# One broadcast tensor_tensor multiply in place of eight tensor_scalar multiplies in a grouped softmax

## The chip, the cores and the metric

One core of one Trainium2 chip. The metric is the device time of one execution in microseconds, lower is better. A profile is one execution taken by the hardware profiler; its span, from first to last instruction, is about 2 us shorter than the device time. A run counts as slow when it takes over 1.5% more than the fastest of the same kernel; the others are called fast. Of a kernel run only once the state is unknown.

## The reference

A softmax over groups: each row of 4352 numbers is eight groups of 544, and each group is normalised by itself.

```python
B, N, D, G = 4, 4096, 4352, 8           # x is float32
def reference(x):
    Dg = D // G                          # 544
    x_g = x.reshape(B, N, G, Dg)
    x_g = x_g - x_g.max(axis=-1, keepdims=True)
    exp = np.exp(x_g)
    out = exp / exp.sum(axis=-1, keepdims=True)
    return out.reshape(B, N, D)
```

Input and output are 285 MB each.

## The kernel before

The 16384 rows are cut into 128 tiles of 128 rows. A tile is loaded by one DMA of 2.2 MB, worked on in place and stored by one DMA. VectorE (DVE) finds the eight maxima, ScalarE (ACT) does the exponentials and their sums, DVE takes the reciprocals and scales. Twelve tile buffers are in use; all transfers go out in order from the queue of SyncE (SP).

```python
NBUF = 12
pool = ctx.enter_context(tc.tile_pool(name="io", bufs=NBUF))
small = ctx.enter_context(tc.tile_pool(name="small", bufs=4))
# ...
def expo(i):
    xt = tiles[i]
    mx = small.tile([P, G], f32, name="mx")
    nc.vector.reduce_max(out=mx, in_=xt, axis=mybir.AxisListType.X, negate=True)   # L45
    # ... eight activations (Exp, bias=mx of the group, accum_out=sm of the group)  # L49

def scale(i):
    xt = tiles[i]
    rs = small.tile([P, G], f32, name="rs")
    nc.vector.reciprocal(out=rs, in_=sums.pop(i))                                   # L61
    for g in range(G):
        nc.vector.tensor_scalar_mul(out=xt[:, g, :], in0=xt[:, g, :], scalar1=rs[:, g:g + 1])  # L63

AHEAD = NBUF - 2
with tc.manual_schedule():
    for i in range(AHEAD):
        load(i)                          # L37
    for i in range(nt + 1):
        if i < nt:
            expo(i)
        if i:
            scale(i - 1)
            store(i - 1, nc.sync)        # L40
            if i - 1 + AHEAD < nt:
                load(i - 1 + AHEAD)
```

## Time and profile before

| | before |
|---|---|
| device time, median of 3 runs | 1342.13 us (1341.66 to 1342.44) |
| span of the profile | 1340.1 us |
| DVE busy | 1046.7 us, 78% |
| ACT busy | 764.3 us, 57% |
| moved | 570.44 MB, 431 GB/s in the steady part |

How to read the lines below. A row of a group of instructions has: source line, engine, operation, output<-input by name, then by shape, count | busy us in all, mean ns of one | idle us of the engine just before them and what ended most of it. The digits after "DMA" are the busy share of the transfer engines in tenths, in 40 equal slices of the span. The lines themselves stand in the prediction.

### The profile page before, as it was taken

To read this page: it belongs to the slowest core of one execution; us is meant where nothing else is said; L and a number is where in the kernel's file an instruction comes from. 1 tells how busy PE (TensorE), PEld (TensorE's weight loads), DVE (VectorE), ACT (ScalarE), POOL (GpSimd) and SP (SyncE) were. 2 spreads that over 40 slices of the span, in tenths; PEclk is the share of its full clock that TensorE was granted. 3 is DMA by queue.
4 is the path that set the end of the run, shared out by engine and by line. 5 is a ranking of instruction groups with operands and counts; after the bars stand their busy time and mean duration, and the time that the engine had idled before them with its cause. 6 is when DMAs were issued, how large, how long until landed. Compare 5 with 4: busy or idle time off the path is not lost.

```text
span 1340.1 us, 4119 instructions
## 1 busy us (share of the span) xinstructions
DVE 1046.7 (78%) x1280; ACT 764.3 (57%) x2049; POOL 0.2 (0%) x4
## 2 busy tenths in 40 slices
DVE  6999987878777887888777877778877887777760
ACT  5777766555655565556555556555665556555540
POOL 0000000000000000000000000000000000000000
DMA  9999999999999999999999999999999999999996
GB/s 399 426 429 431 430 430 432 432 432 431 431 432 430 432 431 432 431 431 431 431 430 431 432 430 432 431 430 431 431 432 430 432 431 429 430 431 431 430 432 266
DMA packets 36896, 570.70 MB, mean 426 GB/s; under 512 B 4096, under 2 KB 4096, under 8 KB 4096
## 3 DMA queue, kind: packets, MB, share of 16 engines
q1 hardware_dynamic: 36864, 570.44, 99.4%
q14 instruction: 32, 0.26, 0.0%
HBM read 285.21 MB, written 285.21 MB: 426 GB/s over the span
## 4 chain that ended last, share of the span: by engine, by line
DMA 88%; DVE 7%; SPq 1%; ACT 1%; issue 1%; DVEq 0%; ACTq 0%
DMA out_dram<-xt 85%; DVE mx L45 4%; DVE xt L63 3%; DMA xt<-in_x_dram 3%; SPq L37 1%; ACT xt L49 1%; DVE rs L61 0%; DVEq L104 0%; ACTq L104 0%
## 5 line engine op out<-in xcount | busy, mean ns | idle before, releaser
L49 ACT ACTIVATE xt<-xt,mx 128x544 f32<-128x544 f32 x1024 | 751.2, 735 | 524.3 <-issue 435.8
L45 DVE TENSOR_REDUCE mx<-xt 128x8 f32<-128x4352 f32 x128 | 599.6, 4685 | 247.6 <-DMA xt<-in_x_dram 247.6
L63 DVE TENSOR_SCALAR xt<-xt,rs 128x544 f32<-128x544 f32 x1024 | 434.2, 498 | 4.5
L49 ACT ACTIVATION_READ_ACCUMULATOR xt<-xt,mx 128x1 f32 x1024 | 191.3, 187 | 0.0
L61 DVE RECIPROCAL rs<-sm 128x8 f32<-128x8 f32 x128 | 24.7, 193 | 3.4 <-ACT xt L49 3.4
L49 ACT ACT_TABLE_LOAD x1 | 1.3, 1283 | 9.9 <-DMA xt<-in_x_dram 9.9
L93 POOL MEMSET const-bfloat16-1.0<- 128x1 bf16 x1 | 0.1, 101 | 0.0
L93 POOL MEMSET const-uint8-127<- 128x1 uint8 x1 | 0.1, 101 | 0.0
L93 POOL MEMSET const-float32-0.0<- 128x1 f32 x1 | 0.1, 98 | 0.2 <-issue 0.2
L93 POOL MEMSET const-float32-1.0<- 128x1 f32 x1 | 0.1, 98 | 0.0
## 6 DMA issues: line engine op xcount, KB each, us to landing
xt<-in_x_dram SPq DMA_DIRECT2D x128, 2176.0 KB, 25.8
out_dram<-xt SPq DMA_DIRECT2D x128, 2176.0 KB, 30.6
```

The lines of the kernel that those rows point to most:

```text
L37: nc.sync.dma_start(out=xt, in_=xg[i * P:(i + 1) * P])
L45: nc.vector.reduce_max(out=mx, in_=xt, axis=mybir.AxisListType.X, negate=True)
L49: nc.scalar.activation(out=xt[:, g, :], in_=xt[:, g, :], func=mybir.ActivationFunctionType.Exp, bias=mx[:, g:g + 1], scale=1.0, accum_out= ...
L61: nc.vector.reciprocal(out=rs, in_=sums.pop(i))
L63: nc.vector.tensor_scalar_mul(out=xt[:, g, :], in0=xt[:, g, :], scalar1=rs[:, g:g + 1])
L93: nc = _bacc.Bacc("TRN2", target_bir_lowering=False, num_devices=1)
```

## The change

The intent is fewer instructions: 128 multiplies in place of 1024. The reciprocals `rs` (128x8) are read as if they were 128x8x544, each repeated along its group.

```diff
-    def scale(i):
-        xt = tiles[i]
+    def scale(i, r):
+        xr = row(i, r)
         rs = small.tile([P, G], f32, name="rs")
-        nc.vector.reciprocal(out=rs, in_=sums.pop(i))
-        for g in range(G):
-            nc.vector.tensor_scalar_mul(out=xt[:, g, :], in0=xt[:, g, :], scalar1=rs[:, g:g + 1])
+        nc.vector.reciprocal(out=rs, in_=sums.pop((i, r)))
+        nc.vector.tensor_mul(
+            out=xr, in0=xr, in1=rs.unsqueeze(2).to_broadcast([P, G, Dg]))
```

The rest of the diff (cut here) rewrites the loops so that a tile could hold several rows a partition. With `R = 1`, as it stands, the tiles, transfers and order are the ones of before.

More of the change, by code (lines that the diff above doesn't have):

```diff
@@ L18 @@
     P = 128
+    R = 1
     NBUF = 12
@@ L23, with rows, store, row @@
     Dg = D // G
-    xg = xf.rearrange("n (g d) -> n g d", g=G)
-    og = of.rearrange("n (g d) -> n g d", g=G)
-    nt = N // P
+    f32 = mybir.dt.float32
     pool = ctx.enter_context(tc.tile_pool(name="io", bufs=NBUF))
     small = ctx.enter_context(tc.tile_pool(name="small", bufs=4))
-    f32 = mybir.dt.float32
+    spans = []
+    at = 0
+    while at < N:
+        r = min(R, (N - at) // P)
+        spans.append((at, r))
+        at += r * P
+    nt = len(spans)
     tiles = {}
     sums = {}
+    def rows(dram, i):
+        at, r = spans[i]
+        return dram[at:at + r * P].rearrange("(p r) d -> p (r d)", r=r)
     def load(i):
-        xt = pool.tile([P, G, Dg], f32, name="xt")
+        xt = pool.tile([P, R * D], f32, name="xt")
         tiles[i] = xt
-        nc.sync.dma_start(out=xt, in_=xg[i * P:(i + 1) * P])
-    def store(i, eng):
-        eng.dma_start(out=og[i * P:(i + 1) * P], in_=tiles.pop(i))
-    def expo(i):
-        xt = tiles[i]
+        nc.sync.dma_start(out=xt[:, :spans[i][1] * D], in_=rows(xf, i))
+    def store(i):
+        nc.sync.dma_start(out=rows(of, i), in_=tiles[i][:, :spans[i][1] * D])
+    def row(i, r):
+        return tiles[i][:, r * D:(r + 1) * D].rearrange("p (g d) -> p g d", g=G)
+    def expo(i, r):
+        xr = row(i, r)
         mx = small.tile([P, G], f32, name="mx")
-        nc.vector.reduce_max(out=mx, in_=xt, axis=mybir.AxisListType.X, negate=True)
+        nc.vector.reduce_max(out=mx, in_=xr, axis=mybir.AxisListType.X, negate=True)
         sm = small.tile([P, G], f32, name="sm")
-        sums[i] = sm
+        sums[i, r] = sm
         for g in range(G):
             nc.scalar.activation(
-                out=xt[:, g, :],
-                in_=xt[:, g, :],
+                out=xr[:, g, :],
+                in_=xr[:, g, :],
                 func=mybir.ActivationFunctionType.Exp,
@@ L56, in expo @@
             )
-    def scale(i):
-        xt = tiles[i]
+    def scale(i, r):
+        xr = row(i, r)
         rs = small.tile([P, G], f32, name="rs")
-        nc.vector.reciprocal(out=rs, in_=sums.pop(i))
-        for g in range(G):
-            nc.vector.tensor_scalar_mul(out=xt[:, g, :], in0=xt[:, g, :], scalar1=rs[:, g:g + 1])
+        nc.vector.reciprocal(out=rs, in_=sums.pop((i, r)))
+        nc.vector.tensor_mul(
+            out=xr, in0=xr, in1=rs.unsqueeze(2).to_broadcast([P, G, Dg]))
     AHEAD = NBUF - 2
+    work = [(i, r) for i in range(nt) for r in range(spans[i][1])]
     with tc.manual_schedule():
@@ L70 @@
             load(i)
-        for i in range(nt + 1):
-            if i < nt:
-                expo(i)
-            if i:
-                scale(i - 1)
-                store(i - 1, nc.sync)
-                if i - 1 + AHEAD < nt:
-                    load(i - 1 + AHEAD)
+        for n in range(len(work) + 1):
+            if n < len(work):
+                expo(*work[n])
+            if n:
+                i, r = work[n - 1]
+                scale(i, r)
+                if r == spans[i][1] - 1:
+                    store(i)
+                    if i + AHEAD < nt:
+                        load(i + AHEAD)
 _INS = ['x']
```

## The prediction

> **What bounds the kernel now.** I read the page first: busy shares, the DMA rows of the 40 slices, the share of the DMA queue, and the chain that ended last.
>
> ```profile
> span 1340.1 us, 4119 instructions
> DVE 1046.7 (78%) x1280; ACT 764.3 (57%) x2049; POOL 0.2 (0%) x4
> DMA  9999999999999999999999999999999999999996
> ...
> q1 hardware_dynamic: 36864, 570.44, 99.4%
> ...
> DMA 88%; DVE 7%; SPq 1%; ACT 1%; issue 1%; DVEq 0%; ACTq 0%
> ...
> L45 DVE TENSOR_REDUCE mx<-xt 128x8 f32<-128x4352 f32 x128 | 599.6, 4685 | 247.6 <-DMA xt<-in_x_dram 247.6
> L63 DVE TENSOR_SCALAR xt<-xt,rs 128x544 f32<-128x544 f32 x1024 | 434.2, 498 | 4.5
> ```
>
> The reader is to see that the transfer engines are full in 39 of 40 slices and that the input and output (570.44 MB) take 99.4% of their time. At the 431 GB/s that the slices show, 570.44 MB are 1323.5 us; start-up and the emptying at the end are the other 17. DVE is busy 78%, and its only large idle item, 247.6 us, is spent waiting for loads: it waits for the transfers, not they for it.
>
> Whether a slower DVE would reach the transfers is decided by the queue that issues them. So next come the waits of that queue (who waited for whom: us in total, times, longest).
>
> ```profile
> SPq L37 <- DMA out_dram<-xt: 1104.5, 116, 16.7
> ...
> SPq L40 <- DVE xt L63: 13.1, 5, 4.1
> ```
>
> A load (L37) waits for the store that frees its buffer, 1104.5 us in all. A store (L40) waited for the multiply only 5 times, 13.1 us: stores are nearly always ready before their turn. How long before, the instructions of one steady tile show (start, duration, in brackets the idle time before):
>
> ```profile
> 598.20 4.69 DVE L45 TENSOR_REDUCE mx<-xt 128x8 f32<-128x4352 f32 x1 [2.08 <-DMA xt<-in_x_dram]
> 602.81 0.19 DVE L61 RECIPROCAL rs<-sm 128x8 f32<-128x8 f32 x1
> ...
> 603.03 3.39 DVE L63 TENSOR_SCALAR xt<-xt,rs 128x544 f32<-128x544 f32 x8
> ...
> 603.36 0.33 SPq L37 DMA_DIRECT2D xt<-in_x_dram  x1
> ...
> 603.74 0.46 SPq L40 DMA_DIRECT2D out_dram<-xt  x1
> ...
> 608.52 4.69 DVE L45 TENSOR_REDUCE mx<-xt 128x8 f32<-128x4352 f32 x1 [2.09 <-DMA xt<-in_x_dram]
> ```
>
> From reduce to reduce a tile takes 608.52 - 598.20 = 10.32 us, which is what the transfers need (2 x 2.228 MB at 431 GB/s = 10.34 us). DVE works 8.2 of them and idles 2.1. Counting the issues from the first one on, the load at 603.36 is that of tile 64 and the store at 603.74 that of tile 55. A load lands 25.8 us after its issue (page, DMA issues), so tile 64 is reduced at about 629.4, three periods after 598.20; the reduce at 598.20 is then tile 61, and the multiply at 603.03 works on tile 60 (each turn reduces a tile, then scales the one before). So tile 55 was scaled five periods before its store was issued: some 48 us of slack. The slack of the reduce is 2.1 us a tile and that of the store 48 us.
>
> **What the Trainium skill says.** (1) "VectorE: DVE Perf Modes", section "The perf-mode tier table": in fp32 from SBUF, tensor_scalar runs at two elements a cycle, tensor_tensor and tensor_reduce at one, since the second tensor takes the second read port. The same page's errata section gives (N+151)/0.96 ns for an fp32 tensor_tensor add. The trace agrees for what it holds: the reduce of 4352 took 4685 ns, against 4690 by that formula; a multiply of 544 took 498 ns, under the 567 that one element a cycle would cost (544/0.96), so it runs in the faster mode. The trace of before has no tensor_tensor. (2) "Perfetto Trace Analysis", section "Optimizing Scalar/DVE Operations": each DVE instruction on SBUF carries some 60 ns, and the profiled latency about twice that. The trace: eight multiplies span 3.39 us, so they start (3390 - 498)/7 = 413 ns apart, of which 283 are elements (544/2/0.96): 130 ns each, closer to the second figure. (3) "SBUF — State Buffer", section "Who interferes with whom": DMA never contends with a compute engine. The trace agrees closely: from 40 to 60 us, with DVE busy 19.93 of 20, the transfers moved 425 GB/s; at 300 to 320, with DVE at 15.75, 430; from 1303 to 1318, with no engine at work, 433. GpSimd, which shares DVE's second port by that page, is idle here.
>
> **The change, part by part.**
> Removed: 1024 multiplies, eight a tile, 8 x 413 ns = 3.31 us of DVE a tile from first start to the next instruction.
> Added: 128 tensor_tensor of 128x4352. Record by the formula (4352+151)/0.96 = 4690 ns. The reduce, with the same count, has the next instruction start 4.59 to 4.61 us after it, so I take 4.60 us on the engine (estimate). Two effects work against each other: seven fixed costs saved (7 x 0.13 = 0.91 us), and twice the cycles for the elements (4352/2/0.96 = 2.27 us more). Net about +1.3 us a tile; 4.60 - 3.31 gives 1.29. Grouping the instructions makes the work slower, because it leaves the fast mode.
> Unchanged: reduce and reciprocal, exponentials on ACT, number, size and order of transfers. In the built programs the loads' waits are the same; a store has gained a wait for the exponentials of its own tile, which end before the multiply does, so it costs nothing beyond one queue entry.
> DVE a tile: 4.60 (reduce) + 0.23 (to the multiply) + 4.60 = 9.43 us, before 8.13. That is under 10.33. Over 128 tiles: 599.6 + 24.7 + 128 x 4.60 = 1213 us, 90% of the span; DVE stays the second, not the first.
> On the path: in the steady part +1.29 comes out of the 2.1 us idle and leaves 0.8, and a store is ready 1.3 us later out of 48. Cost 0.
> Ramp: DVE begins behind the loads and works back to back. Before, tile k's reduce starts near 24.1 + 8.13(k-2), and its load lands near 88.7 + 10.33(k-12) (the load of tile 12 was issued at 62.93); these meet at k = 20, 167 us. The trace has the first such wait of more than a microsecond ending at 172.49. After: 25.4 + 9.43(k-2), which meets it at k = 46 or so, 440 us. The store of tile 3 was issued at 63.35; its multiply will now end near 53.7, and the margin grows with each tile. The first three stores go out 1 to 3.5 us later, with at least seven transfers of 5.2 us still queued ahead: no hole. Cost 0.
> Tail: the last load lands at 1287.75, the last store was issued at 1302.2 and will be at 1303.5. Transfers stay at full rate till 1324, so about four stores are queued when it comes: hidden too. The last 14 us are a few transfer engines ending late, at a fifth of the rate. Cost 0 to 1.3 us.
> Sum: 0 to +1.3 us. There may be a trifle to gain from fewer instruction fetches (0.26 MB in all). I predict 1342.3 us.
>
> **The rivals.**
> Fewer instructions, faster kernel: for it, 896 fewer records on DVE. Against it, those hide behind a full DMA, and were they all free, the floor of 1323.5 us plus the fill would still stand: less than 1% to win. Time 1339 to 1342.
> DVE becomes the bound: it needs a tensor_tensor above 10.33 - 4.83 = 5.5 us, 1.2 cycles an element. A broadcast that rereads one word 544 times, or two read streams in SBUF, might cost that; no row of before shows such an operand, and the tier table gives one a cycle. At two cycles an element, 9.1 us, a tile would take 13.9 us and the kernel some 1800.
> A wait takes the place of the removed one: a late multiply holds the store, which holds the load behind it in the same queue. Against it stand the 48 us of slack and the five waits. If it did bite in the ramp: 1345 to 1350.
> The tail shows in full: 1343.4.
> DVE's second read stream slows the transfers: with DVE at 90% at the 425 GB/s of the busiest window instead of 431, 1% or 13 us, 1355. But that window is also the ramp, where loads outnumber stores, so I give it little.
>
> **Range and chances.** The three runs of before lie within 0.8 us, so the range is about mechanism: 1339.5 (rival one) to 1346 (tail and a little of the ramp). The chance of slower by over 2% is that of a tensor_tensor above 5.7 us or so: 0.03. Faster by 2% would need more than the transfers leave: 0.01. Within 2%: 0.96.
>
> **What would show it.** Right: the tensor_tensor's row at about 4.69 us mean; DVE near 90%; the reduce's idle time down from 247.6 to some 80 us (82 tiles x 0.85 and the start); its waits beginning near 440 us; DMA still at 9 in 39 slices and 430 GB/s; stores still not waiting for DVE after the first few. Wrong: a mean above 5.5 us with the reduce never waiting; a dip in GB/s between 20 and 70 us (ramp); mid-span GB/s below 428 (contention); or a mean near 2.4 us, were the fast mode kept, in which case DVE idles more and the time is the same.

## The result, and the profile after

The changed kernel took 1341.01 us (median of 4 runs, 1339.41 to 1341.88) against 1342.04 us for the kernel before (4 runs). The ratio is 0.9991, with a 95% interval of 0.9974 to 1.0008: the same. The profiled run is the fastest of the four. A ratio here is the mean time of one kernel's fast runs over that of the other's of the same rounds, so it is not quite the ratio of the medians.

The page of the changed kernel: span, busy engines, transfers by slice, the transfer queue, the chain that ended last, and the two big groups on DVE.

```profile
span 1337.6 us, 3339 instructions
...
DVE 1210.8 (91%) x384; ACT 764.3 (57%) x2049; POOL 0.2 (0%) x4
...
DMA  9999999999999999999999999999999999999996
...
q1 hardware_dynamic: 36864, 570.44, 99.6%
...
DMA 83%; DVE 11%; issue 2%; ACT 1%; SPq 1%; ACTq 0%
...
L58 DVE TENSOR_REDUCE mx<-xt 128x8 f32<-128x4352 f32 x128 | 599.6, 4684 | 83.7 <-DMA xt<-in_x_dram 83.7
L75 DVE TENSOR_TENSOR xt<-xt,rs 128x4352 f32<-128x4352 f32 x128 | 600.6, 4692 | 4.4
```

The multiplies went from 434.2 to 600.6 us: 166 us more work on DVE, from an eighth of the instructions. The reduce's wait for loads went from 247.6 to 83.7 us, 164 us less. The work was paid out of that wait, and the transfers are as full as before.

One steady tile of the changed kernel, in order of time (start, duration, in brackets the idle time before):

```profile
598.46 4.69 DVE L58 TENSOR_REDUCE mx<-xt 128x8 f32<-128x4352 f32 x1 [1.48 <-DMA xt<-in_x_dram]
603.07 0.19 DVE L74 RECIPROCAL rs<-sm 128x8 f32<-128x8 f32 x1
603.29 4.69 DVE L75 TENSOR_TENSOR xt<-xt,rs 128x4352 f32<-128x4352 f32 x1
603.62 0.33 SPq L47 DMA_DIRECT2D xt<-in_x_dram  x1
604.04 0.41 SPq L50 DMA_DIRECT2D out_dram<-xt  x1
608.78 4.69 DVE L58 TENSOR_REDUCE mx<-xt 128x8 f32<-128x4352 f32 x1 [0.80 <-DMA xt<-in_x_dram]
```

The tile still takes 10.32 us from reduce to reduce, and the load and the store go out 0.3 us from where they did before. Only the idle time shrank: 0.80 us before the second reduce, where it was 2.09.

The waits of the queue that issues the transfers (who waited for whom: us in all, times, longest):

```profile
SPq L47 <- DMA out_dram<-xt: 1103.4, 116, 16.6
SPq L50 <- DVE xt L75: 41.9, 5, 10.2
```

Stores waited for the multiply as often as before, 5 times, if for longer (13.1 us became 41.9). Three of the five are the first stores (the other two come after 1280 us, at the very end), which went out at 25.66, 35.07 and 44.51 us in place of 24.23, 32.37 and 41.04. The load that waits for the first of them to land, that of tile 12, went out at 62.92 us, before at 62.93: nothing was lost.

### The profile page after: what moved, and what is told of

It is laid out like the page before. It is cut to its first block, busy times and chain, and to the rows that moved or that the text cites. A ratio compares the mean times of both kernels' runs of the same rounds, so it can differ in the third digit from the quotient of the medians.

```text
span 1337.6 us, 3339 instructions
## 1 busy us (share of the span) xinstructions
DVE 1210.8 (91%) x384; ACT 764.3 (57%) x2049; POOL 0.2 (0%) x4
## 4 chain that ended last, share of the span: by engine, by line
DMA 83%; DVE 11%; issue 2%; ACT 1%; SPq 1%; ACTq 0%
DMA out_dram<-xt 80%; DVE xt L75 6%; DVE mx L58 5%; DMA xt<-in_x_dram 3%; ACT xt L62 1%; SPq L47 1%; DVE rs L74 0%; SPq L50 0%; ACTq L120 0%
## 5 line engine op out<-in xcount | busy, mean ns | idle before, releaser
L58 DVE TENSOR_REDUCE mx<-xt 128x8 f32<-128x4352 f32 x128 | 599.6, 4684 | 83.7 <-DMA xt<-in_x_dram 83.7
L75 DVE TENSOR_TENSOR xt<-xt,rs 128x4352 f32<-128x4352 f32 x128 | 600.6, 4692 | 4.4
```

The lines of the kernel that those rows point to most:

```text
L58: nc.vector.reduce_max(out=mx, in_=xr, axis=mybir.AxisListType.X, negate=True)
L75: nc.vector.tensor_mul(out=xr, in0=xr, in1=rs.unsqueeze(2).to_broadcast([P, G, Dg]))
```

## The experiments

The theory: the change makes DVE slower by about 1.3 us a tile, and this costs nothing for two reasons together. DVE still needs less a tile (9.43 us) than the transfers (10.33), and with 12 buffers a multiply that ends later does not move the issue of a transfer. The rivals: the multiply does cost time and the rewritten loops give it back; the room is nearly used up; throughput alone decides and the buffers do not matter. Twelve kernels were run. All gave the right result except one. The edits are shown cut: where a scratch tile is used, the lines that create it are left out.

### The multiply alone

```diff
-        for g in range(G):
-            nc.vector.tensor_scalar_mul(out=xt[:, g, :], in0=xt[:, g, :], scalar1=rs[:, g:g + 1])
+        nc.vector.tensor_mul(
+            out=xt, in0=xt, in1=rs.unsqueeze(2).to_broadcast([P, G, Dg]))
```

> The kernel before with nothing changed but the multiply (one tensor_tensor of 128x4352 in place of eight tensor_scalar; none of the rewritten loops or access patterns). Theory (the DVE is slower by 1.29 us a tile and all of it is hidden): within 0.3% of before, 1339 to 1343 us, DVE busy 1205 to 1215 us. Rival (the rewritten loops and transfers gave back what the multiply cost): this one alone would be slower than the full change, by up to 128 x 1.29 = 165 us and at least a few us. Five rounds, to see whether the 0.1% gain of the full change is real.

1339.66 us (5 runs, 1338.79 to 1340.50) against 1341.44 for before; ratio 0.9986, interval 0.9974 to 0.9999. DVE was busy 1210.8 us, as in the full change. The multiply alone does what the full change does, so the rewritten loops give nothing back. That rival is out.

### How much more DVE work is free

Extra multiplies of 128x512 on a scratch tile, once or twice a tile, after the scaling:

```diff
+    junk = extra.tile([P, 512], f32, name="junk")
+        nc.vector.tensor_mul(out=junk, in0=junk, in1=junk)     # in scale(), one or two of these
```

> The changed kernel with one more DVE instruction a tile (a 128x512 tensor_tensor on a scratch tile, about 0.60 us from start to next start). DVE then needs 9.43 + 0.60 = 10.03 us a tile, still under the 10.33 of the transfers. Theory (all hidden while DVE is under the transfers' period): same, 1339 to 1344 us, the reduce's idle time nearly gone, DVE busy about 97%. Rival (the hiding is nearly used up and a busy DVE starts to delay stores): slower by 0.5% or more, up to 1.5%.

1340.83 us (4 runs), ratio 0.9994, interval 0.9979 to 1.0009: free. DVE was busy 96% of the span, and the reduce waited for loads only 13.4 us in all, 9.0 of it in the first 20 us. At 10.03 us a tile (reduces at 597.99, 608.02 and 618.06) DVE catches up with the loads only at 1130 us; until then no reduce after the first two waits for a load. So for most of the run this is not a DVE that waits 0.3 us a tile, but one still behind the loads, and even that costs nothing: its stores waited for the multiply 5 times, as before.

> The changed kernel with two more such instructions a tile, the second waiting for the first: 0.72 + 0.60 = 1.32 us, so 10.75 us a tile, over the 10.33 of the transfers. Theory: DVE becomes the bound; reduces start at 26.8 + 10.75(k-2), the last at about 1371, the last multiply ends near 1386, its store lands some 7.5 us later: 1395 us (1385 to 1405), slower by 4%; the reduce never waits for loads after the start; mid-span transfer rate down to about 415 GB/s. Rival (DVE's busy share does not matter because transfers run ahead with 12 buffers): same.

1396.32 us (4 runs, 1396.25 to 1396.42), ratio 1.0408, interval 1.0394 to 1.0422. From the page of this kernel: the transfer rate in the 40 slices (GB/s), and the reduce's group.

```profile
GB/s 400 428 428 430 431 429 430 432 431 431 431 431 431 431 431 432 431 431 432 432 426 414 416 415 412 414 418 414 411 416 414 416 415 409 417 416 413 280 192 256
...
L58 DVE TENSOR_REDUCE mx<-xt 128x8 f32<-128x4352 f32 x128 | 598.8, 4678 | 8.7 <-DMA xt<-in_x_dram 8.7
```

The reduce never waits after the start: DVE is the bound, at 10.76 us a tile (reduces at 898.07, 908.83 and 919.59 us). The transfers still run at 431 GB/s for half of the span and then fall to some 415 (2 x 2.228 MB in 10.76 us is 414). They live first on the tiles that were scaled ahead: from 200 to 300 us 6 stores waited for the multiply, from 400 us on nearly every one. After that they live on the transfers already issued, of which five stood in the queue at 200 us and 1.4 at 700 (issues less landed bytes). Here one sees the room of the buffers being drained: in this run a DVE that is 0.4 us a tile too slow goes unnoticed by the transfers for some 700 us.

> The kernel before with the same two extra instructions a tile as the run e3_after_two: 8.13 + 1.32 = 9.45 us a tile, under 10.33. Theory: same as before, 1340 to 1344 us. Against e3_after_two this shows that the change has spent 1.29 us a tile of room: the same extra work is free before the change and costs some 50 us after it.

1342.80 us (4 runs), ratio 1.0007, interval 0.9992 to 1.0022. The same extra work that costs the changed kernel 4% costs the kernel before nothing. So the change did spend something real, 1.3 us a tile of room, although its own time does not show it.

### Fewer buffers

```diff
-    NBUF = 12
+    NBUF = 4        # or 5; loads are issued NBUF - 2 tiles ahead
```

> The kernel before with 4 buffers instead of 12, so loads are issued 2 tiles ahead instead of 10. The load of tile n+1 then goes out only after tile n-1 is scaled, behind its store: each tile pays issue 0.7 + store and load 12.3 us + reduce 4.6 + 0.23 + multiplies 3.4 = 21.3 us. Expected 2730 us (2400 to 2900), DVE busy under 45%.

> The changed kernel with 4 buffers. Theory of buffers (the cost is hidden by the room that 12 buffers give between a multiply and the issue of its store): with that room gone, 1.29 us a tile shows in full, 165 us more than e5_before_nb4 (145 to 185, 6%), though DVE is busy only some 45% of the time. Rival (throughput alone: the cost is hidden as long as DVE needs less a tile than the transfers): no difference between the two, since DVE is far from full in both.

2691.67 us before and 2861.28 after the change (4 runs each, all within 2 us): 169.6 us more, or 1.33 a tile; their ratios to the kernel before are 2.0073 and 2.1338. The reduce's group of the two pages, before and then after the change:

```profile
L45 DVE TENSOR_REDUCE mx<-xt 128x8 f32<-128x4352 f32 x128 | 599.8, 4686 | 1625.5 <-DMA xt<-in_x_dram 1625.5
```

```profile
L58 DVE TENSOR_REDUCE mx<-xt 128x8 f32<-128x4352 f32 x128 | 599.8, 4686 | 1630.9 <-DMA xt<-in_x_dram 1630.9
```

DVE waits more than 1600 us for loads in both, yet its slower multiply shows in full. This idle time is no room. The order of one tile shows why, here in the changed kernel with 4 buffers:

```profile
1318.48 4.69 DVE L75 TENSOR_TENSOR xt<-xt,rs 128x4352 f32<-128x4352 f32 x1
1323.23 0.34 SPq L50 DMA_DIRECT2D out_dram<-xt  x1
1323.62 0.43 SPq L47 DMA_DIRECT2D xt<-in_x_dram  x1
1335.99 4.69 DVE L58 TENSOR_REDUCE mx<-xt 128x8 f32<-128x4352 f32 x1 [12.83 <-DMA xt<-in_x_dram]
```

The store goes out 0.06 us after the multiply ends, the load behind it, and the reduce starts when that load has landed. The idle 12.83 us begins only when the multiply ends; a longer multiply moves it, it does not shorten it. The rival of throughput alone is out. The queue of transfers says the same. With 12 buffers 5 of the changed kernel's 128 stores waited for the multiply; with 5 and with 4 buffers all of them did:

```profile
SPq L50 <- DVE xt L75: 1336.6, 128, 23.7
SPq L50 <- DVE xt L75: 2739.3, 128, 23.6
```

> The kernel before with 5 buffers, loads 3 tiles ahead. Two tiles then share one turn of load, reduce, multiply: 2 T = 0.8 + 12.3 + 8.2, T = 10.65 us, just above the transfers' 10.33: 1390 us (1350 to 1430).

> The changed kernel with 5 buffers. Buffers theory: T = (21.3 + 1.29)/2 = 11.3 us, so half of 1.29 a tile shows: 83 us more than e7_before_nb5 (40 to 110), DVE idle 1.9 us a tile all the same. Throughput alone: no difference.

1387.00 us before and 1458.61 after the change (4 runs each): 71.6 us more, 0.56 a tile, about half of 1.3 as the theory has it, and inside its 40 to 110. DVE still waited 228.3 us for loads in the changed one, and it was busy 83% of the span, less than the 91% it has with 12 buffers, where the change is free. A busy share does not tell whether a slower engine costs time.

### Instruction count and mode taken apart

```diff
-        nc.vector.tensor_mul(
-            out=xr, in0=xr, in1=rs.unsqueeze(2).to_broadcast([P, G, Dg]))
+        nc.vector.tensor_scalar_mul(out=xr, in0=xr, scalar1=rs[:, 0:1])
```

This gives a wrong result: all groups are scaled by the first group's reciprocal.

> Wrong result on purpose: the changed kernel with its tensor_tensor replaced by one tensor_scalar of 128x4352 with the first group's reciprocal alone. It takes apart the two effects on DVE: one instruction, but in the fast mode. Theory (130 ns fixed cost an instruction, two elements a cycle for tensor_scalar): 2.27 us of elements plus the 0.21 us that a record has beyond its elements, 2.48 us mean; DVE a tile 4.59 + 0.23 + 2.4 = 7.2 us; time the same as before, 1338 to 1344. Rival (the tensor_tensor is slow for its size, not for its mode): near 4.69 us.

1341.73 us (one run, state unknown). The multiply's group:

```profile
L75 DVE TENSOR_SCALAR xt<-xt,rs 128x4352 f32<-128x4352 f32 x128 | 318.3, 2486 | 4.5
```

2486 ns where 2480 was expected. One tensor_scalar over the tile occupies DVE 2.41 us (it starts at 42.24 and the next reduce at 44.65), eight take 3.31, one tensor_tensor 4.61. So joining eight instructions saves 0.90 us, and leaving the mode of two elements a cycle costs 2.20. The first effect is the intent of the change, the second its price. Between 544 and 4352 elements the record of a tensor_scalar grows from 498 to 2486 ns, 0.52 ns an element; that of a tensor_tensor, from 692 at 512 to 4692 at 4352, 1.04.

The 512 is the extra multiply of the section before, which has no broadcast operand:

```profile
L78 DVE TENSOR_TENSOR junk<-junk 128x512 f32<-128x512 f32 x128 | 88.6, 692 | 4.5
```

This answers the rival that rereading one word 544 times is what costs: the multiply with the broadcast fits the one without it at the 1.04 ns an element that the reduce, which has no second operand, also takes (4685 ns for 4352).

### Where the last microsecond comes from

The changed kernel's median was 1 us below before, and runs until then ended later the more instruction packets they fetched. Idle GpSimd got tiny instructions to raise that number (129 turns of the loop, so 4128 in the first run and 1032 in the second):

```diff
+            for _ in range(32):                # 8 in the second run
+                nc.gpsimd.memset(dot, 1.0)     # one word a partition, once a tile
```

> The changed kernel with 32 tiny memsets of one word a partition for each tile on the idle GpSimd engine (4096 instructions more, nothing else). It tests where the last 1 to 3 us come from: runs so far end later the more instruction packets they fetch (26: 1339.7 and 1341.0; 27: 1340.8; 32: 1341.4 and 1342.0; 34: 1342.8), and at the end a few transfer engines finish 10 to 14 us after the rest. Theory (the fetches of 8 KB, 0.3 to 0.5 us each, load the engines that end last): 58 packets in place of 26, end later by 4 to 12 us, 1344 to 1353. Rival (run-to-run spread): within 1.5 us of the changed kernel.

Not settled. One of six runs took 1348.91 us, the others 1379 to 1399 and count as slow, although the granted clock was 1.00 in each. In the profiled run, a slow one, the rate fell from 431 GB/s to some 400 at about 590 us, while the transfer engines stayed full; neither expectation has that. The last memset ended at 645 us, and the rate stayed low to the end, so neither running memsets nor their fetches can be what held it down then; the eleven runs of the kernel before beside it were all fast. The cause is open, and it is no evidence on the change, whose runs are all fast.

> A quarter of the dose of e10_pool_instr, which gave one run at 1348.9 us and five between 1379 and 1399: 8 tiny GpSimd memsets a tile, 1024 instructions, so some 34 instruction packets in place of 26. Theory (the fetches delay the transfer engines that end last, about 0.25 us a packet by the one fast run of e10): 2 us later than the changed kernel run beside it, 1342.5 to 1344, and no run above 1350. Rival (fetches do not matter, and e10's slow runs have another cause, the memsets themselves): within 0.7 us of the changed kernel, or again some runs above 1360.

1339.49 us (5 runs, 1338.78 to 1340.25), ratio 0.9988, interval 0.9975 to 1.0002, with 1032 instructions more. It was not 2 us later than the changed kernel beside it, but 1.7 us earlier in the medians, which is more than the rival's 0.7 too and within the spread of runs. The theory of the fetches falls, at least for fetches by this engine at this number.

> The changed kernel once more, unaltered, beside e11 and the kernel before, on one chip. If the small gain seen so far (ratio 0.9991 for it, 0.9986 for the multiply alone) is real: 0.9980 to 0.9995 with an interval that leaves out 1. If it was spread: 0.9995 to 1.0005.

1341.15 us (5 runs, 1339.99 to 1342.76), ratio 1.0000, interval 0.9987 to 1.0012. The gain of 0.1% did not show again: on this chip it can't be told from the spread of runs. Over all chips the 14 runs with the one multiply (the change, the multiply alone and this run) lie 0.8 us below the mean of the 40 of before; whether that little is real stays open.

## Why the prediction was right

The time lies 1.3 us below the predicted 1342.3, inside the range of 1339.5 to 1346. The sum of 0 to +1.3 us is what runs can't tell from zero, so the time alone proves little; the steps do. By its steps:

- The cost of the multiply. 4690 ns was estimated, 4692 measured; 4.60 us on the engine, 4.61 measured (388.78 to the next reduce at 393.39, in the ramp, the stretch in which DVE has not yet caught up with the loads). The +1.29 us a tile is 1.30, and with 4 buffers 1.33 in the time itself.
- DVE a tile: 9.43 us predicted; back-to-back reduces at 383.96 and 393.39 give 9.43. DVE busy 1210.8 us against 1213 (the prediction's sum adds the reduce by its record and the multiply by the spacing of starts, which makes it a little too high).
- The idle of the reduce: "some 80 us", measured 83.7. It was said to begin near 440 us; the first waits after the start are 0.18 us at 431.39 and 0.79 us at 441.71.
- No store held up for the multiply in the steady part: of the five waits three lie before 100 us and two after 1280. At the first three stores fewer transfers stood in the queue than the "at least seven" of the prediction: issues less landed bytes give 5.6 to 6.0 in the trace, which was still enough. The runs with 4 and 5 buffers show that it is this room that makes the change free.
- Tail (after the last load): the last store was expected at 1303.5 us and went out at 1301.1, because the last load had landed 2.5 us sooner in this run. From the last reduce to it, 14.4 us became 15.8: 1.4 us, hidden as expected, since the transfers were full until 1324.
- Contention: the rival of slower transfers asked for less than 428 GB/s in mid-span. From 300 to 320 us DVE was busy 19.93 of 20 and the transfers moved 430, as with the less busy DVE of before. From 20 to 70 us the rate was 425 against 428: if that is the change, it is worth 50 x 3/428 = 0.35 us. In the profiles of the multiply alone and of the repeated run it was 426 and 427, so it may be spread.
- The rival in which DVE becomes the bound did not come true. The threshold it named, 10.33 us a tile, lies between two runs: the one with 10.76 is bound by DVE and the one with 10.03 is not slower.

One thing the prediction had not foreseen is how the chain that ended last reads. With the single extra multiply, at the same time of 1340.83 us, the share of DVE in that chain jumps:

```profile
DVE 48%; issue 25%; DMA 23%; ACT 1%; SPq 0%; DVEq 0%; ACTq 0%
```

In the kernel before it was DMA 88%. The chain follows whatever came last at each step, and when DVE and the transfers are nearly level it can run along either; it does not say how much would be saved.

## What to carry to other kernels

Before trading many small instructions for one, look up whether the one keeps the fast mode: here seven saved starts (0.9 us) did not pay for half the rate (2.2 us). A change that makes an engine slower was free here only while two things held, that the engine stayed under the bound's period and that its results were ready ahead of their use; read the second from the waits of the queue that uses them, not from the busy share. And a change that leaves the time alone may still have spent room that the next change will need: the same extra work was free before this one and cost 4% after it.

## What the Trainium skill lacked or had wrong

- "VectorE: DVE Perf Modes", "The TRN2 errata": its formula for an fp32 tensor_tensor is given for an add, checked at 512 and 2048 elements. With 4352 elements and a second operand that repeats each word 544 times it held too: 4692 ns measured, 4690 by the formula. No page gives a time for such an operand in fp32.
- "Perfetto Trace Analysis", "Optimizing Scalar/DVE Operations": the 60 ns that a DVE instruction occupies the engine beyond its elements fit the reduce (4.59 - 4.53 = 0.06 us) and, nearly, the tensor_tensor (4.61 - 4.53 = 0.08), but not the tensor_scalar in its fast mode: 413 - 283 = 130 ns with 544 elements and 2.41 - 2.27 = 0.14 us with 4352. The prediction set the 130 ns beside the page's figure for the latency; as a spacing of starts it belongs beside the 60. No page says that a tensor_scalar has about twice the fixed cost; whether the fast mode or the scalar operand brings it, no run here tells.
- No page explains the slow runs of the kernel with 4128 tiny GpSimd memsets: five of six were 2 to 4% slower than the sixth at a granted clock of 1.00, in the profiled one with the transfer rate down from 431 to some 400 GB/s from 590 us on and after the last memset too. That the memsets are the cause is not shown.
